# mLSTM output part on pairs of chunks, and the output projection in steps of 24 products

## The chip, the cores and the metric

The kernel runs on one core of one Trainium2 chip. The metric is device time in microseconds (us) of one execution, as the median of several runs. The five engines appear in the profile as PE (TensorE's matmuls) and PEld (its weight loads), DVE (VectorE), ACT (ScalarE), POOL (GpSimd) and SP (SyncE, which here only issues DMAs).

## What is computed

One encoder layer for two sequences, 2048 and 256 tokens, with model width 1024 and float32 data. An RMSNorm and one input projection feed two groups of heads: eight bidirectional mLSTM heads and eight attention heads (grouped, with two key heads). Their outputs stand side by side and pass through the output projection `w_out`, with a residual. Then follow a second norm, an up projection, a width-3 convolution, a gate and a down projection.

```python
x = x + jnp.concatenate([m_out, a_out], axis=-1) @ w_out
h = rmsnorm(x, norm2_w)
u = centred_dwconv(h @ w_up, conv_w, conv_b)
a, g = jnp.split(u, 2, axis=-1)
return x + (jax.nn.silu(g) * a) @ w_down
```

The change lies in the mLSTM heads. Per head and direction, with decay weights `Dw` inside a chunk and a carried state `C`, `n`:

```python
s = jnp.einsum('bhld,bhsd->bhls', qb, kb) * Dw
num = iw[..., None] * jnp.einsum('bhld,bhde->bhle', qb, C) + jnp.einsum('bhls,bhse->bhle', s, vb)
den = iw * jnp.einsum('bhld,bhd->bhl', qb, n) + jnp.sum(s, axis=-1)
h = num / jnp.maximum(jnp.abs(den), jnp.exp(-m_t))[..., None]
```

The two directions are added, each head is normalised by its root mean square, scaled, and multiplied by a sigmoid gate.

## The kernel before

Float32 products are made from two parts of each operand (a rounded high part and the rest), so one product of the text is three on TensorE. "Products" below are these single matmul instructions on 128 x 128 weights.

Tokens are cut into 18 chunks of 128 (`NT`) and 9 blocks of 256 (`NB`), so a block is a pair of chunks. `phase_a` (L139) norms the tokens and projects the attention heads, `gate_math` (L338) prepares the mLSTM gates. Then `run_both` (L1474) runs two Python generators against each other: `attention` (L430) and `mlstm` (L637). Each `yield` hands over a weight, and `run_both` takes the next step from the side that is behind by these weights. This gives the order in which instructions are emitted. The framework then orders them for each engine by priority (the place of emission, less the offset of a `high_priority` region) and by what is ready in its own timeline; on the chip every engine runs its instructions in that order.

`mlstm` goes over four pairs of heads, p = 0 to 3. For each, `proj_steps` (L846) makes keys, queries, values and gate of the nine blocks, two steps of 48 products each for a block, and writes the gate to `og_d`; `upd` (L751) makes the state increments, `recur` (L765) chains them over the chunks on VectorE, and `out_steps` (L862) makes the outputs. The output steps of pair p alternate with the projection steps of pair p + 1. For the last pair (p = `LASTP` = 3), the query and gate projection of a block, `proj_qo` (L725), is made inside `out_steps`, at every second chunk; its gate goes to one of three `ogT` tiles (`OTB`).

The output part of a chunk i has four pieces, all emitted at `high_priority` with an offset of 2000 (`MPRI`), but for the first:
- `out_a` (L774): GpSimd issues a DMA that broadcasts the chunk's row of `nm_d` into the tile `dm`, masks both directions with `affine_select` (L782), and ScalarE takes four exponentials of 128 x 128 (L785). For p < 3 it also loads the gate of a block (L790).
- `out_b` (L794): the score product `pS` (L799), two VectorE products with `dm` (L802), the state product `pI` (L805) and its scaling into `s1` (L808).
- `out_c` (L811): the value product `pN` (L817), added to `s1` (L818), three small denominator operations (L820 to L822), the normalisation (L823), the sum over directions into `hh` (L826), two squares on ScalarE that also overwrite part of `s1` (L829), the reciprocal root on GpSimd (L98, L99), the product with it (L831) and the gate (L833).
- `out_d` (L835): a transpose (L838), a scaled copy on ScalarE (L841; for p = 3 a product with the gate on VectorE, L843) and a DMA to `mix_d` (L844).

Step i of `out_steps` emits `out_d` of chunk i - 6, `out_c` of i - 2, `out_b` of i - 1 and `out_a` of i. There are three `dm` tiles (`DMB`), two `s1` tiles (`S1B`), six `hh` tiles (`DLAG`), and two PSUM banks (`MB`) for all small mLSTM products.

When `mlstm` has ended, its tiles are released and `phase_c` (L902), the output projection, is the second generator: four steps load and split `w_out`; then, for each block, four "z-steps" make 48 products each (`mm`, L935) and add the residual (`post`, L945). The norm of a block (`tail`, L953) is emitted at the first z-step of the next one. One step is taken at each attention step (`CSTEP`), and a block begins only when attention has finished its tokens (`g.mixed`). From then on attention is emitted at `high_priority` with an offset of 1000 (`APRI`). When attention has ended, the remaining steps of `phase_c` are run alone (L1455), and each of them releases one of seven preparations of the up projection: four sums of `n2` (`n2_sums`, L1023) and three operand loads (`n2_load`, L1001). The last block's norm is emitted after the first products of the up projection (L1466).

Of the kernel before, what the change touches and what calls it, by code (L numbers as in the profile page):

```python
# [9 lines left out]
F32 = mybir.dt.float32  # L10
F32R = mybir.dt.float32r
AF = mybir.ActivationFunctionType
ALU = mybir.AluOpType
# [4 lines left out]
P = 128  # L18
# [4 lines left out]
NT = T // P  # L23
# [5 lines left out]
NEG = -1e30  # L29
# [8 lines left out]
NB = T // BT  # L38
# [7 lines left out]
LASTP = 3  # L46
OW3 = 3
OTB = 3
# [8 lines left out]
RST = 512  # L57
QZB = 2
RWM = 4
S1B = 2  # L60
DMB = 3
KWB = 2
CSTEP = 1
TDVE = 6
# [15 lines left out]
P0 = ((V, V),) * 4  # L80
P1 = ((V, V),) * 7
LOP = ()
DLAG = 6
SEGS = ((0, NT1), (NT1, NT))


# [8 lines left out]
def rstd_of(g, pool, ms, n, name):  # L95
    nc = g.nc
    r = pool.tile([P, n], F32, tag="rstd", name=name)
    nc.gpsimd.tensor_scalar(r, ms, EPS, None, ALU.add)  # L98
    nc.gpsimd.tensor_tensor(r, r, g.mhalf[:, 0:n], ALU.pow)  # L99
    return r  # L100
# [536 lines left out]
def mlstm(g, tc, s1, sp, sw, sn, pj_, pm):  # L637


    nc = g.nc  # L640
# [3 lines left out]
    tm = g.tm  # L644
# [129 lines left out]
    def out_a(s, i):  # L774
        nm = f"{s.p}_{i}"
        o = Pair()
        o.dm = sp.tile([P, 2, 2, P], F32, tag="dm", name="dm" + nm, bufs=DMB)
        nc.gpsimd.dma_start(o.dm.rearrange("p d h l -> p (d h l)"),
                          g.nm_d[i, 4 * s.p:4 * s.p + 4].rearrange("r l -> (r l)").unsqueeze(0).to_broadcast([P, 4 * P]))
        for d in range(2):  # L780
            sgn = 1 - 2 * d
            nc.gpsimd.affine_select(out=o.dm[:, d], in_=o.dm[:, d], compare_op=ALU.is_ge, fill=NEG, base=0,  # L782
                                    pattern=[[0, 2], [sgn, P]], channel_multiplier=-sgn)
            for h in range(2):
                nc.scalar.activation(o.dm[:, d, h], o.dm[:, d, h], AF.Exp,  # L785
                                     bias=tm[:, i, 0, d, 2 * s.p + h:2 * s.p + h + 1])
        if s.p < LASTP:
            if i % 2 == 0:
                s.og = s1.tile([P, 2, P], F32, tag="ogT", name="ogr" + nm, bufs=OTB)
                nc.gpsimd.dma_start(s.og, g.og_d[s.p, i // 2])  # L790
            o.og = s.og[:, i % 2]
        return o

    def out_b(s, i, o):  # L794
        nm = f"{s.p}_{i}"
        pS = pm.tile([P, 2, P], F32, tag="m", name="mS" + nm)
        t = slice((i % 2) * P, (i % 2) * P + P)
        q = s.qb[i // 2][:, i % 2]
        nc.tensor.matmul(pS.rearrange("p h t -> p (h t)"), s.kT[i // 2][:, t], q.rearrange("p h t -> p (h t)"),  # L799
                         start=True, stop=True)  # L800
        for d in range(2):
            nc.vector.tensor_tensor(o.dm[:, d], o.dm[:, d], pS, ALU.mult)  # L802
        pI = pm.tile([P, 2, 2, 65], F32, tag="m", name="mI" + nm)
        for h in range(2):
            nc.tensor.matmul(pI[:, h].rearrange("p d e -> p (d e)"), q[:, h, :],  # L805
                             s.C[i].rearrange("p d e -> p (d e)"), start=True, stop=True)
        o.s1 = sp.tile([P, 2, 2, 65], F32, tag="s1", name="s1" + nm, bufs=S1B)
        nc.vector.tensor_tensor(o.s1, pI.rearrange("p h d e -> p d h e"),  # L808
                                tm[:, i, 2, :, s.hs].unsqueeze(3).to_broadcast([P, 2, 2, 65]), ALU.mult)

    def out_c(s, i, o):  # L811
        nm = f"{s.p}_{i}"
        s1 = o.s1
        pN = pm.tile([P, 2, 2, 65], F32, tag="m", name="mN" + nm)
        for d in range(2):
            for h in range(2):
                nc.tensor.matmul(pN[:, d, h, :], o.dm[:, d, h, :], s.va[i // 2][:, i % 2, h, :], start=True, stop=True)  # L817
        nc.vector.tensor_tensor(s1, pN, s1, ALU.add)  # L818
# [3 lines left out]
        nc.vector.reciprocal(dn, dn)  # L822
        nc.vector.tensor_tensor(s1[:, :, :, 0:64], s1[:, :, :, 0:64],  # L823
                                dn.unsqueeze(3).to_broadcast([P, 2, 2, 64]), ALU.mult)
        hh = o.hh = sp.tile([P, 2, 64], F32, tag="hh", name="hh" + nm, bufs=DLAG)
        nc.vector.tensor_tensor(hh, s1[:, 0, :, 0:64], s1[:, 1, :, 0:64], ALU.add)  # L826
        ms = sp.tile([P, 2], F32, tag="mms", name="mms" + nm, bufs=4)
        for h in range(2):
            nc.scalar.activation(s1[:, 0, h, 0:64], hh[:, h, :], AF.Square, scale=0.125, accum_out=ms[:, h:h + 1])  # L829
        r = rstd_of(g, sp, ms, 2, "mr" + nm)  # L830
        nc.vector.tensor_tensor(hh, hh, r.unsqueeze(2).to_broadcast([P, 2, 64]), ALU.mult)  # L831
        if s.p < LASTP:
            nc.vector.scalar_tensor_tensor(hh, o.og.rearrange("p (h d) -> p h d", h=2), 1.0, hh, ALU.add, ALU.mult)  # L833

    def out_d(s, i, o):  # L835
        nm = f"{s.p}_{i}"
        pT = pm.tile([P, P], F32, tag="m", name="mT" + nm)
        nc.tensor.transpose(pT, o.hh.rearrange("p h d -> p (h d)"), g.ident)  # L838
        mx = sp.tile([P, P], F32, tag="mmx", name="mmx" + nm, bufs=2)
        if s.p < LASTP:  # L840
            nc.scalar.activation(mx, pT, AF.Copy, scale=mhw[:, s.p:s.p + 1])  # L841
        else:
            nc.vector.tensor_tensor(mx, pT, s.og[i // 2][:, (i % 2) * P:(i % 2) * P + P], ALU.mult)  # L843
        (nc.scalar if s.p < LASTP else nc.sync).dma_start(g.mix_d[i // 2, :, s.p, (i % 2) * P:(i % 2) * P + P], mx)  # L844

    def proj_steps(s):  # L846
        for b in range(NB + 2):
# [14 lines left out]
    def out_steps(s):  # L862
        os_ = {}
        s.og = {}
        for i in range(NT + DLAG):
            if s.p == LASTP and i % 2 == 0 and i < NT:
                proj_qo(s, i // 2)
            if DLAG <= i:
                with tc.high_priority(offset=MPRI):
                    out_d(s, i - DLAG, os_.pop(i - DLAG))  # L870
            if 2 <= i < NT + 2:
                with tc.high_priority(offset=MPRI):
                    out_c(s, i - 2, os_[i - 2])
            if 1 <= i < NT + 1:
                with tc.high_priority(offset=MPRI):
                    out_b(s, i - 1, os_[i - 1])
            if i < NT:
                os_[i] = out_a(s, i)
            yield (2.7 if s.p < LASTP else OW3) if i < NT else 1

    s = weights(0)
    yield from proj_steps(s)
    for p in range(4):
# [3 lines left out]
        if p < 3:  # L887
# [4 lines left out]
            while True:  # L892
                a, b = next(outs, None), next(ps, None)
# [3 lines left out]
            s = s2  # L897
# [4 lines left out]
def phase_c(g, sn, sp, pp, wps):  # L902
# [3 lines left out]
    nc = g.nc  # L906
# [28 lines left out]
    def mm(b, z, mx):  # L935
        po = pp.tile([P, 2, BT], F32, tag="po", name=f"po{b}_{z}")
        for o in range(2):
            n = slice(((2 * z + o) % 4) * P, ((2 * z + o) % 4 + 1) * P)
            for c in range(NCC):
                for k, (a, h) in enumerate(((0, 0), (0, 1), (1, 0))):  # L940
                    nc.tensor.matmul(po[:, o], wo[c][z // 2][:, a, n], mx[c][:, h, :],  # L941
                                     start=(c == 0 and k == 0), stop=(c == NCC - 1 and k == 2))
        return po

    def post(b, z, x, po, acc):  # L945
# [22 lines left out]
    for b in range(NB):  # L968
        yield 2 * b
        x, mx = loads(b)  # L970
        for z in range(4):
            po = mm(b, z, mx)
            if z == 0:
                if prev is not None:
                    tail(*prev)
                acc = sp.tile([P, 2, BT], F32, tag="acc", name=f"cacc{b}", bufs=1)
            post(b, z, x, po, acc)
            if z < 3:
                yield None
        prev = (b, x, acc)  # L980
# [576 lines left out]
```

## Time and profile before

| what | value |
|---|---|
| median of 3 runs | 3376.03 us (3375.04 to 3377.26) |
| the profiled execution | 3379.7 us |
| its span, first to last instruction | 3378.0 us |
| mean granted TensorE clock | 0.988 |
| VectorE busy, whole span | 2453.2 us (73%) |
| mLSTM output part: first `pS` product, last store | 430.0 us, 1432.6 us |
| output projection: first and last product | 1437.9 us, 1870.6 us |

A row of a group names line, engine, operation, output and inputs, shape and count; after the first bar stand its busy us and the mean ns of one instruction, after the second the idle time of its engine just before it and what ended that. A row of waits names the waiting engine and line, then what released it: us in total, how often, the longest. In a timeline row stand the start, the duration, engine and line. Matmuls overlap on TensorE: one of 512 columns is shown as some 400 ns, though the next begins after 230 ns.

### The profile page before, as it was taken

To read this page: it belongs to the slowest core of one execution; us is meant where nothing else is said; L and a number is where in the kernel's file an instruction comes from. 1 tells how busy PE (TensorE), PEld (TensorE's weight loads), DVE (VectorE), ACT (ScalarE), POOL (GpSimd) and SP (SyncE) were. 2 spreads that over 40 slices of the span, in tenths; PEclk is the share of its full clock that TensorE was granted. 3 is DMA by queue.
4 is the path that set the end of the run, shared out by engine and by line. 5 is a ranking of instruction groups with operands and counts; after the bars stand their busy time and mean duration, and the time that the engine had idled before them with its cause. 6 is when DMAs were issued, how large, how long until landed. Compare 5 with 4: busy or idle time off the path is not lost.

```text
span 3378.0 us, 53454 instructions
## 1 busy us (share of the span) xinstructions
PE 3270.3 (97%) x19566; PEld 3035.8 (90%) x19566; DVE 2453.2 (73%) x3659; ACT 1989.0 (59%) x3706; POOL 692.6 (21%) x1072
## 2 busy tenths in 40 slices
PE   7989999999999999999999899999999999999998
PEld 6778888888888888788878899999999999999998
DVE  7874576666657668876665899998889888666664
ACT  4535666666566776655554555676667667554543
POOL 7774133322215323211112100000000000010201
PEclk9999999999999999999999999999999999999999
DMA  8766343343337343343225756677666657867663
GB/s 246 216 182 193 103 122 94 108 129 96 99 101 217 119 130 118 102 147 99 84 83 158 266 208 219 213 250 264 236 228 240 213 193 258 315 231 274 218 233 122
DMA packets 394551, 601.69 MB, mean 178 GB/s; under 512 B 31248, under 2 KB 255536, under 8 KB 394288
## 3 DMA queue, kind: packets, MB, share of 16 engines
q1 hardware_dynamic: 361232, 553.43, 49.0%
q0 software_dynamic: 11600, 33.04, 3.7%
q10 hardware_dynamic: 21456, 11.80, 1.2%
q8 instruction: 154, 2.52, 0.3%
q14 instruction: 109, 0.89, 0.1%
HBM read 434.23 MB, written 163.92 MB: 177 GB/s over the span
## 4 chain that ended last, share of the span: by engine, by line
PE 73%; issue 7%; ACT 5%; DVE 5%; POOL 5%; DMA 4%; SPq 0%; POOLq 0%; ACTq 0%; DVEq 0%
PE pa L1091 16%; PE pc L1091 8%; PE pf L1347 6%; PE po L941 5%; PE pb L1091 4%; PE mj L681 4%; PE ph L1347 3%; PE mv L691 3%; PE ps L553 3%; PE pv L570 3%; PE pv L572 3%; PE ps L554 2%; PE pv L571 2%; PE px L530 2%; PE pg L1347 2%
## 5 line engine op out<-in xcount | busy, mean ns | idle before, releaser
L559 DVE TENSOR_TENSOR xx<-pe,xx 128x1024 fp32r<-128x1024 f32 x260 | 322.9, 1242 | 193.6 <-ACT xx L558 191.9
L557 ACT ACTIVATE pe<-ps 128x1024 f32<-128x1024 f32 x260 | 266.1, 1023 | 225.2 <-PE ps L554 216.2
L532 DVE TENSOR_REDUCE mx<-px 128x1 f32<-128x1024 f32 x256 | 309.8, 1216 | 93.9 <-PE px L530 92.7
L1305 POOL TENSOR_TENSOR sq<-sq,sq 128x384 f32<-128x384 f32 x38 | 48.7, 1282 | 1397.6 <-ACT sq L1301 1315.8
L558 ACT ACTIVATE xx<-pe 128x1024 fp32r<-128x1024 f32 x260 | 274.9, 1058 | 6.3 <-PE pv L572 1.3
L941 PEld LDWEIGHTS po<-cmx,wo 128*128 128x128 f32 x1728 | 228.6, 191 | 18.2 <-ACT cmx L928 2.1
L941 PE MATMUL po<-cmx,wo 128*128 128x256 f32 x1728 | 235.8, 283 | 1.4 <-ACT cmx L928 1.1
L1095 ACT ACTIVATE u<-pa 128x386 f32<-128x386 f32 (+2 forms) x264 | 129.2, 489 | 177.7 <-PE pa L1091 176.4
L553 PE MATMUL ps<-qq,kk 128*128 128x512 f32 x520 | 214.4, 412 | 13.7 <-ACT pe L557 10.4
L570 PE MATMUL pv<-xx,vv 128*128 128x512 f32 x520 | 214.3, 412 | 13.7 <-ACT rs L580 7.8
L572 PE MATMUL pv<-xx,vv 128*128 128x512 f32 x520 | 212.6, 409 | 2.9 <-DVE xx L559 2.8
L571 PE MATMUL pv<-xx,vl 128*64 128x512 f32 x520 | 209.6, 403 | 0.0
L554 PE MATMUL ps<-qm,kl 65*128 65x512 f32 x520 | 208.5, 401 | 0.4 <-ACT qm L545 0.4
L681 PEld LDWEIGHTS mj<-mn,wm 128*128 128x128 f32 x1296 | 177.9, 193 | 16.8 <-ACT og L695 3.9
L691 PE MATMUL mv<-wm,mn 128*128 128x256 f32 x1296 | 192.2, 286 | 0.8 <-ACT qb L687 0.8
L681 PE MATMUL mj<-mn,wm 128*128 128x256 f32 x1296 | 190.2, 288 | 2.8 <-ACT og L695 2.4
L227 PE MATMUL pj<-w_a,n1T 128*128 128x512 f32 (+1 forms) x864 | 179.1, 362 | 10.7 <-DVE n1T L185 6.3
L691 PEld LDWEIGHTS mv<-wm,mn 128*128 128x128 f32 x1296 | 175.9, 190 | 14.1 <-ACT qb L687 1.4
L227 PEld LDWEIGHTS pj<-w_a,n1T 128*128 128x128 f32 x864 | 144.4, 196 | 31.0 <-DVE n1T L185 7.2
L530 PE MATMUL px<-kk,qq 128*128 128x512 f32 x512 | 165.9, 405 | 5.4 <-ACT pe L557 4.5
L785 ACT ACTIVATE dm<-dm,tm 128x128 f32<-128x128 f32 x288 | 95.0, 392 | 107.5 <-POOL dm L782 103.2
L1091 PE MATMUL pc<-nt,wb 128*128 128x386 f32 (+2 forms) x792 | 148.4, 341 | 4.8 <-ACT nt L1015 3.3
(325 smaller groups left out, 8314.5 us busy)
## 6 DMA issues: line engine op xcount, KB each, us to landing
mn<-n_d SPq DMA_DIRECT2D x216, 256.0 KB, 3.2
ru<-w_up SPq DMA_DIRECT2D x88, 512.0 KB, 5.1
rs<-wsu_d SPq DMA_DIRECT2D x88, 512.0 KB, 5.5
act_d<-ts SPq DMA_DIRECT2D x33, 768.0 KB, 5.8
nt<-act_d SPq DMA_DIRECT2D x60, 384.0 KB, 4.9
re_t<-wsd_d SPq DMA_DIRECT2D x45, 512.0 KB, 5.0
wsu_d<-tw SPq DMA_DIRECT2D x44, 512.0 KB, 3.9
act_d<-ya SPq DMA_DIRECT2D x99, 192.0 KB, 3.0
```

The lines of the kernel that those rows point to most:

```text
L227: nc.tensor.matmul(pjs[t][:, c0:c1], nTs[tiles[t]][:, c, a, :], ws[c][:, b, c0:c1], start=(c == 0 and k == 0), stop=(c == NCC - 1 and k == 2))
L532: nc.vector.tensor_reduce(s.mx[:, t0, z0:z0 + 1], ps, AX.X, ALU.max)
L553: nc.tensor.matmul(o, kk[:, kc:kc + P], s.qq, start=True, stop=False)
L559: nc.vector.tensor_tensor(x[:, 1], pe, f32(x[:, 0]), ALU.subtract)
L570: nc.tensor.matmul(s.pv, vv[:, kt % 4, :], x1, start=kt == 0, stop=False)
L571: nc.tensor.matmul(s.pv[0:HD], vl[:, kt % 4, :], x1, start=False, stop=False)
L572: nc.tensor.matmul(s.pv, vv[:, kt % 4, :], x2, start=False, stop=kt == s.nk - 1)
L681: nc.tensor.matmul(pj[:, o], s.w[c][:, a, o * P:(o + 1) * P], nT[c][:, h, :], start=(c + o + k == 0), stop=(c == NCC - 1 and k == 2 and o ...
L691: nc.tensor.matmul(pv[:, o], nT[c][:, a, o * P:(o + 1) * P], s.w[c][:, h, 256:512], start=(c + o + k == 0), stop=(c == NCC - 1 and k == 2 ...
L941: nc.tensor.matmul(po[:, o], wo[c][z // 2][:, a, n], mx[c][:, h, :], start=(c == 0 and k == 0), stop=(c == NCC - 1 and k == 2))
L1091: s.nc.tensor.matmul(p, w[:, aa, c, :], ops[k][:, c, bb, 0:s.n], start=c == 0 and i == 0 and not add, stop=c == NCC // 2 - 1 and i == 2, s ...
L1347: nc.tensor.matmul(ps[c], w[:, aa, c, :], t[:, gi - g0, bb, 0:H], start=gi == 0 and m == 0 and not more, stop=gi == NG - 1 and m == 2, ski ...
```

## The change

The four pieces of the output part take a block b (two chunks) where they took a chunk:
- `out_a`: `dm` holds two chunks; one DMA and one `affine_select` for each direction, over both chunks; eight exponentials as before; the gate load of the block.
- `out_b`: both chunks' `pS` products go to one bank, and one VectorE product of 1024 columns takes all of `dm`; `pI` and its scaling stay two.
- `out_c`: `pN` and its addition stay two; the denominator, normalisation, sum over directions, reciprocal root, product and gate are one operation each for the block; four squares as before.
- `out_d`: two transposes into one bank, one copy (or product) and one DMA of 256 columns.

Buffers: `s1` one of double size (was two), `dm` two of double size (were three), `hh` two of double size (were six), `mmx` one of double size (was two). `out_steps` emits `out_a` and, for p = 3, `proj_qo` of block 0 ahead of its loop; in a block's first half step `out_d` of j - 2, then `proj_qo` of j + 1, then `out_c` of j - 1; in its second half step `out_b` of j and `out_a` of j + 1. It yields twice per block with the weights as before (2.7, or 3 for the last pair), and with 1 in the two steps at the end.

In `phase_c`, `mm` yields after the first of its two groups of 24 products, so a block is handed out in eight steps.

```diff
-S1B = 2
-DMB = 3
+S1B = 1
+DMB = 2
-DLAG = 6
+DLAG = 2
...
-        for d in range(2):
-            nc.vector.tensor_tensor(o.dm[:, d], o.dm[:, d], pS, ALU.mult)
+        dm = o.dm.rearrange("p d i h l -> p d (i h l)")
+        nc.vector.tensor_tensor(dm, dm, pS.rearrange("p i t -> p (i t)").unsqueeze(1).to_broadcast([P, 2, 4 * P]),
+                                ALU.mult)
...
-        dn = sp.tile([P, 2, 2], F32, tag="dn", name="dn" + nm, bufs=4)
-        nc.vector.scalar_tensor_tensor(dn, s1[:, :, :, 64], -1.0, s1[:, :, :, 64], ALU.mult, ALU.max)
-        nc.vector.tensor_tensor(dn, dn, tm[:, i, 3, :, s.hs], ALU.max)
+        dn = sp.tile([P, 2, 2, 2], F32, tag="dn", name="dn" + nm, bufs=2)
+        nc.vector.scalar_tensor_tensor(dn, s1[:, :, :, :, 64], -1.0, s1[:, :, :, :, 64], ALU.mult, ALU.max)
+        nc.vector.tensor_tensor(dn, dn, tm[:, 2 * b:2 * b + 2, 3, :, s.hs], ALU.max)
         nc.vector.reciprocal(dn, dn)
...
-        for i in range(NT + DLAG):
-            if s.p == LASTP and i % 2 == 0 and i < NT:
-                proj_qo(s, i // 2)
+        last = s.p == LASTP
+        if last:
+            proj_qo(s, 0)
+        os_[0] = out_a(s, 0)
+        for j in range(NB + DLAG):
+            w = (OW3 if last else 2.7) if j < NB else 1
+            if DLAG <= j:
+                with tc.high_priority(offset=MPRI):
+                    out_d(s, j - DLAG, os_.pop(j - DLAG))
+            if last and j + 1 < NB:
+                proj_qo(s, j + 1)
+            if 1 <= j <= NB:
+                with tc.high_priority(offset=MPRI):
+                    out_c(s, j - 1, os_[j - 1])
+            yield w
+            if j < NB:
+                with tc.high_priority(offset=MPRI):
+                    out_b(s, j, os_[j])
+            if j + 1 < NB:
+                os_[j + 1] = out_a(s, j + 1)
+            yield w
...
                     nc.tensor.matmul(po[:, o], wo[c][z // 2][:, a, n], mx[c][:, h, :],
                                      start=(c == 0 and k == 0), stop=(c == NCC - 1 and k == 2))
+            if o == 0:
+                yield None
         return po
...
-            po = mm(b, z, mx)
+            po = yield from mm(b, z, mx)
```

More of the change, by code (lines that the diff above doesn't have):

```diff
@@ L792, in out_a @@
[L792 to L800, printed above, removed]
-        for d in range(2):
[L802 to L818, printed above, removed]
-        dn = sp.tile([P, 2, 2], F32, tag="dn", name="dn" + nm, bufs=4)
-        nc.vector.scalar_tensor_tensor(dn, s1[:, :, :, 64], -1.0, s1[:, :, :, 64], ALU.mult, ALU.max)
-        nc.vector.tensor_tensor(dn, dn, tm[:, i, 3, :, s.hs], ALU.max)
[L822 to L839, printed above, removed]
+            nc.gpsimd.affine_select(out=o.dm[:, d].rearrange("p i h l -> p (i h) l"),
+                                    in_=o.dm[:, d].rearrange("p i h l -> p (i h) l"), compare_op=ALU.is_ge, fill=NEG,
+                                    base=0, pattern=[[0, 4], [sgn, P]], channel_multiplier=-sgn)
@@ new lines, in out_a, with out_b @@
+            for i in range(2):
+                for h in range(2):
+                    k = 2 * s.p + h
+                    nc.scalar.activation(o.dm[:, d, i, h], o.dm[:, d, i, h], AF.Exp, bias=tm[:, i0 + i, 0, d, k:k + 1])
+        if s.p < LASTP:
+            o.og = s1.tile([P, 2, P], F32, tag="ogT", name="ogr" + nm, bufs=OTB)
+            nc.gpsimd.dma_start(o.og, g.og_d[s.p, b])
+        return o
+    def out_b(s, b, o):
+        nm = f"{s.p}_{b}"
+        pS = pm.tile([P, 2, 2 * P], F32, tag="m", name="mS" + nm)
+        for i in range(2):
+            nc.tensor.matmul(pS[:, i], s.kT[b][:, i * P:(i + 1) * P], s.qb[b][:, i].rearrange("p h t -> p (h t)"),
+                             start=True, stop=True)
+        dm = o.dm.rearrange("p d i h l -> p d (i h l)")
+        nc.vector.tensor_tensor(dm, dm, pS.rearrange("p i t -> p (i t)").unsqueeze(1).to_broadcast([P, 2, 4 * P]),
+                                ALU.mult)
+        o.s1 = sp.tile([P, 2, 2, 2, 65], F32, tag="s1", name="s1" + nm, bufs=S1B)
+        for i in range(2):
+            pI = pm.tile([P, 2, 2, 65], F32, tag="m", name=f"mI{nm}_{i}")
+            for h in range(2):
+                nc.tensor.matmul(pI[:, h].rearrange("p d e -> p (d e)"), s.qb[b][:, i, h, :],
+                                 s.C[2 * b + i].rearrange("p d e -> p (d e)"), start=True, stop=True)
+            nc.vector.tensor_tensor(o.s1[:, i], pI.rearrange("p h d e -> p d h e"),
+                                    tm[:, 2 * b + i, 2, :, s.hs].unsqueeze(3).to_broadcast([P, 2, 2, 65]), ALU.mult)
@@ L840, in out_d @@
+    def out_d(s, b, o):
+        nm = f"{s.p}_{b}"
+        pT = pm.tile([P, 2, P], F32, tag="m", name="mT" + nm)
+        for i in range(2):
+            nc.tensor.transpose(pT[:, i], o.hh[:, i].rearrange("p h d -> p (h d)"), g.ident)
+        mx = sp.tile([P, 2, P], F32, tag="mmx", name="mmx" + nm, bufs=1)
         if s.p < LASTP:
```

59 lines of the change are left out of this document (35 added, 24 removed).

## The prediction

> **What bounds the kernel now.** I read the page first (engine shares), then busy time by stretch (windows), the waits of TensorE, the groups by line, and last the timelines around the places where TensorE stands idle.
>
> ```profile
> span 3378.0 us, 53454 instructions
> PE 3270.3 (97%) x19566; PEld 3035.8 (90%) x19566; DVE 2453.2 (73%) x3659; ACT 1989.0 (59%) x3706; POOL 692.6 (21%) x1072
> ```
>
> TensorE is busy 97% of the span, so the whole kernel has 3378.0 - 3270.3 = 108 us in which it shows no work, and every term below is a share of that. The change touches the mLSTM stage (430 to 1437 us) and the output projection beside and behind attention (1437 to 1906 us). The columns of the next rows are the stretch, its length, then busy us of PE, PEld, DVE, ACT and POOL, the granted clock, and the share and GB/s of the DMA engines.
>
> ```profile
> 430.00:1220.00 790.00, 775.00 (x4882) 676.03 (x4881) 539.77 (x1020) 507.09 (x1187) 252.24 (x491) 0.99 0.38 117
> 1220.00:1437.00 217.00, 210.20 (x1263) 177.97 (x1262) 166.48 (x348) 145.48 (x329) 63.76 (x110) 0.99 0.40 121
> ...
> 1280.00:1330.00 50.00, 46.95 (x264) 38.92 (x262) 42.02 (x95) 33.01 (x78) 19.62 (x35) 0.97 0.32 92
> 1405.00:1455.00 50.00, 43.02 (x206) 30.86 (x204) 45.02 (x80) 39.06 (x73) 8.35 (x14) 1.00 0.41 131
> ...
> 1437.00:1630.00 193.00, 188.67 (x1228) 166.60 (x1227) 128.91 (x176) 105.87 (x161) 31.48 (x31) 1.00 0.36 119
> 1630.00:1656.00 26.00, 22.89 (x103) 17.21 (x102) 19.36 (x26) 13.18 (x17) 2.55 (x4) 0.87 0.30 97
> 1656.00:1736.00 80.00, 80.00 (x534) 71.76 (x533) 48.01 (x63) 42.01 (x60) 13.51 (x13) 1.00 0.25 81
> 1736.00:1806.00 70.00, 57.51 (x243) 41.45 (x242) 41.40 (x51) 43.82 (x59) 7.37 (x12) 0.91 0.16 46
> ...
> 1866.00:1906.00 40.00, 30.46 (x158) 29.08 (x157) 33.09 (x47) 18.71 (x25) 8.06 (x5) 0.83 0.93 327
> ```
>
> TensorE's idle time, length less busy: 15.0 + 6.8 = 21.8 us in the mLSTM stage; 4.3 + 3.1 + 0 + 12.5 = 19.9 us while attention runs beside the output projection; 9.5 us at the hand-over to the up projection. Where attention has products of another kind beside it (1656 to 1736) TensorE has no gap at all. Where it has none (1405 to 1455, 1736 to 1806) it loses 14% and 18%. So the ordinary products are filler, and the time is set by where filler is missing and by attention's own chain of waits there:
>
> ```profile
> PE ps L553 <- ACT pe L557: 5.1, 10, 1.6
> PE pv L570 <- ACT rs L580: 4.4, 5, 2.1
> PE px L530 <- ACT pe L557: 3.1, 3, 1.9
> PE pv L570 <- ACT xx L558: 2.5, 5, 0.7
> PE pv L572 <- DVE xx L559: 1.5, 4, 0.7
> ```
>
> These are TensorE's longest waits from 430 to 1437 us (total, times, longest). ScalarE ends most of them; VectorE directly ends 1.5 us. That already says that taking work off VectorE can't return its full amount.
>
> **VectorE, ScalarE and GpSimd work that is merged.** Rows of the operations concerned (busy us, mean ns of one after the bar):
>
> ```profile
> L559 DVE TENSOR_TENSOR xx<-pe,xx 128x1024 fp32r<-128x1024 f32 x260 | 322.9, 1242 | 193.6 <-ACT xx L558 191.9
> ...
> L802 DVE TENSOR_TENSOR dm<-dm,mS 128x256 f32<-128x256 f32 x144 | 53.6, 413 | 15.9 <-PE mS L799 15.0
> L823 DVE TENSOR_TENSOR s<-s,dn 128x256 f32<-128x256 f32 x72 | 31.0, 431 | 1.4
> L818 DVE TENSOR_TENSOR s<-mN,s 128x260 f32<-128x260 f32 x72 | 30.3, 420 | 12.3 <-PE mN L817 12.0
> L831 DVE TENSOR_TENSOR hh<-hh,mr 128x128 f32<-128x128 f32 x72 | 23.9, 331 | 47.3 <-POOL mr L99 45.7 <-ACT qb L687 1.0
> L826 DVE TENSOR_TENSOR hh<-s 128x128 f32<-128x128 f32 x72 | 22.9, 318 | 1.3
> L833 DVE SCALAR_TENSOR_TENSOR hh<-ogr,hh 128x128 f32<-128x128 f32 x54 | 16.1, 297 | 1.0
> L822 DVE RECIPROCAL dn<-dn 128x4 f32<-128x4 f32 x72 | 12.4, 172 | 1.3
> L946 DVE TENSOR_TENSOR cx<-po,cx 128x512 f32<-128x512 f32 x36 | 24.7, 686 | 31.0 <-PE po L941 30.9
> ...
> L829 ACT ACTIVATE s<-hh 128x64 f32<-128x64 f32 x144 | 35.2, 247 | 22.7 <-DVE hh L826 22.5
> L829 ACT ACTIVATION_READ_ACCUMULATOR s<-hh 128x1 f32 x144 | 27.3, 189 | 0.0
> ```
>
> For one pair of chunks of one head pair, of which there are 9 x 4 = 36: four dm products of 413 ns become one of 1024 columns, 1242 ns by the row of the same width, saving 410. The three small denominator operations stand twice each before; by the reciprocal's 172 ns they save 3 x 172 = 516. The normalisation (431 twice) becomes 512 columns, 686 ns: 176. The sum of directions (318 twice), the rstd product (331 twice) and the gate (297 twice; the last head pair has an output product there instead, taken alike) become 256 columns each, 425 ns as an estimate between the 413 and 431 of that width: 211, 237 and 169. The 420 ns operations on pI and pN stay two each. Sum 1.72 us, times 36 = 62 us of VectorE's 2453. [...]
>
> ScalarE keeps the eight exponentials per pair and the four squares; only out_d's copies merge, under 10 us in all. GpSimd's masks cover twice the columns in half the number, and two rstd operations per pair go; GpSimd is 21% busy and stays off the path. The dm loads stay two per pair with equal bytes, and the stores to mix_d halve in number. TensorE's products are the same, so it gains only idle time.
>
> What are 62 us of VectorE worth? At most TensorE's 21.8 us of idle, plus stalls too short to show beside pipelined products; at least nothing. The two stretches where VectorE is nearly full, 42.02 and 45.02 of 50 us, hold 3.0 + 7.0 = 10 us of that idle. I take half of it, 5 us, because attention's own operations fill the rest of VectorE there, and a quarter of the other 11.8, 3 us. **-8 us** (0 to -15).
>
> **The new order of the output part.** The last head pair's query and gate projection is handed out earlier: its ninth block now has 3 x 4 + 4 = 16 units of weight behind it (two steps of the block, two of the next, four of weight 1) where it had 2 x 3 + 6 = 12. A unit is 217 / 60 = 3.6 us, so the stretch without projection products before the output projection starts grows by some 14 us.
>
> ```profile
> L707 PE MATMUL mv<-mvn,wm x432: 274/283/472, 1219.7 to 1399.6; 128*128 128x256 f32 x144
> ...
> L941 PE MATMUL po<-cmx,wo x1728: 274/281/580, 1437.9 to 1870.6; 128*128 128x256 f32 x192
> ```
>
> Today that stretch lasts from 1400 to 1438 us, and it loses at the 14% worked out above: 14 us x 14% = **+2 us** (0 to +5).
>
> **The output projection in steps of 24.** Beside attention I take **0** (-12 to +4). The order on TensorE is not in blocks of 48 today:
>
> ```profile
> 1485.82 1.48 PE L941 MATMUL po<-cmx,wo 128*128 128x256 f32 x11
> 1487.14 0.62 PE L530 MATMUL px<-kk,qq 128*128 128x512 f32 x2
> 1487.60 1.47 PE L941 MATMUL po<-cmx,wo 128*128 128x256 f32 x11
> ```
>
> It is dealt out product by product into attention's gaps, because attention is emitted at a priority 1000 instructions ahead, and handing out smaller pieces changes nothing where it is filler already. The gates on finished attention tiles stay.
>
> Behind attention the hand-out does matter: the remaining steps each release one of seven preparations of the up projection (four n2 sums, three loads). Twice as many steps per block means these come at half the spacing, and begin some four z-steps earlier.
>
> ```profile
> 1812.70 0.93 SPq L1031 DMA_DIRECT2D rn<-n_d  x2
> ...
> 1852.39 1.31 SPq L1031 DMA_DIRECT2D rn<-n_d  x2
> ...
> 1870.60 0.37 SPq L1014 DMA_DIRECT2D nt<-n2t_d  x1
> ...
> PE rs_c L135 <- POOL rcol_c L133: 3.7, 1, 3.7
> PE pc L1091 <- ACT nt L1015: 3.3, 1, 3.3
> ```
>
> The sums now run from 1813 to 1852 us and the load behind them is issued at 1871, when the first up products already stand on TensorE. An earlier start would let those products fill the 3.7 us wait for the last norm. The 3.3 us wait is for a tile whose space is freed by that norm, and stays. **-3 us** (-7 to +2, since the sums then meet the loads of the last two blocks on SP's queue).
>
> **Sum.** -8 + 2 + 0 - 3 = -9 us. The profiled execution took 3379.7 us (1.7 outside the span), 3.7 above the median of the runs, 3376.03. 3379.7 - 9 = 3370.7 profiled, so **3367 us** as a median. 0.2%, 6.8 us, is about what a measurement of this kernel can tell from no change.
>
> **Rivals.** First: VectorE's relief is worth nothing, since ScalarE ends the waits, and the longer stretch takes back the little that the hand-over gives: 0 + 2 + 0 - 3 = -1, 3375 us. For it speaks the list of waits; against it, that VectorE is 84 to 90% busy just where TensorE idles.
>
> Second: the finer hand-out spreads the filler so that it lasts through 1630 to 1656 and 1736 to 1806, 3.1 + 12.5 us of idle. Four blocks take 16 attention steps before and 32 after, nearly the 36 steps of four head blocks. If 12 us of that come back: -9 - 12 = -21, 3355 us. The runs of eleven products speak against it.
>
> Third, slower: the single s1 buffer and the two pair-wide dm buffers make the output part one serial chain. The first write of s1 must wait for the four squares of the pair before, 4 x (247 + 189) = 1.74 us, and those for its whole VectorE chain: 1242 + 4 x 420 + 516 + 686 + 425 = 4.5 us, stretched by attention's operations in front of each. The last head pair's projection depends on this chain through the gate buffers. The pace there is 217 / 9 = 24 us for a pair, and the bare chain 6 us, so it decides only where queueing makes it three to four times as long. Then 100 us run as 1405 to 1455 does, at 14%: +14, with the tail's +2 and no gain elsewhere +16, 3392 us. A single wait is there today:
>
> ```profile
>   ACT s L829: 2.5, 2
> ```
>
> That is VectorE's idle time before s1's write, 2.5 us in two cases. [...]
>
> **Chances.** My forecast (3358 to 3369, faster) 0.39; the second rival 0.13, also faster: 0.52. The first, no change: 0.26. The third 0.22. The range leaves out the worst of the second and the upper part of the third: 3346 to 3390.
>
> **What would show it.** Right: the merged dm product near 1.24 us x36 and VectorE's busy time down by some 60 us; TensorE's products unchanged; its idle time from 430 to 1437 us falling from 21.8 to about 14, with the projection's last product some 10 us earlier relative to the first output product; the n2 sums done before 1840 and no 3.7 us wait at the hand-over. Wrong: runs of output products clearly shorter or longer than today and a filled stretch before attention's end (second rival); VectorE waiting on the squares dozens of times, or the output part's start-to-end growing (third); the same idle time with a lighter VectorE (first).

## The result, and the profile after

The changed kernel takes **3396.17 us** (median of 6 runs, 3391.09 to 3405.32). Beside it the kernel before took 3375.54 us (6 runs, 3374.30 to 3377.26). The ratio is 1.0063, with a 95% interval of 1.0049 to 1.0077: it is slower by some 20 us. I forecast 3367 us, faster, so the sign was wrong. The profiled execution took 3393.13 us, 13.4 more than the profiled one of before; the terms below are made against it.

The page after, its span and engines:

```profile
span 3391.4 us, 52630 instructions
PE 3275.4 (97%) x19566; PEld 3039.5 (90%) x19566; DVE 2415.5 (71%) x3299; ACT 1986.9 (59%) x3679; POOL 647.8 (19%) x928
```

VectorE has 37.7 us less to do and GpSimd 45, as the merge meant. Yet TensorE's idle time over the span, 3391.4 - 3275.4 = 116.0 us, is 8.3 more than before, and with the same 19566 products its busy time is 5.1 more. By stretch, with the columns of the prediction's rows:

```profile
430.00:1220.00 790.00, 765.86 (x4823) 670.08 (x4822) 502.76 (x746) 496.03 (x1147) 222.70 (x382) 0.98 0.41 117
1220.00:1437.00 217.00, 208.22 (x1254) 176.83 (x1253) 152.18 (x250) 140.63 (x328) 49.38 (x73) 0.98 0.42 119
```

In the mLSTM stage TensorE now idles 24.1 + 8.8 = **32.9 us** where it idled 21.8, and its granted clock is lower too. From 1437 to 1950 it idles 30.2 us after and 30.0 before, so the loss belongs to the stage before the output projection. TensorE's and VectorE's and ScalarE's waits in that stage (430 to 1437 us) show its kind. These are waits of the profile after:

```profile
PE pv L570 <- ACT rs L580: 6.3, 4, 2.4
...
PE mu L760 <- DVE s L812: 2.6, 1, 2.6
PE mT L849 <- DVE hh L840: 2.5, 3, 1.6
PE mT L849 <- DVE hh L843: 1.9, 1, 1.9
...
DVE s L823 <- PE mN L822: 40.4, 29, 5.6
DVE s L812 <- ACT s L836: 32.8, 12, 6.4
...
ACT dm L791 <- POOL dm L785: 90.5, 39, 7.0
```

The waits of TensorE that VectorE ends come to 12.7 us in the whole list after, and to 4.0 in the whole list of before (the five rows of the prediction show 1.5 of these). VectorE waits for the squares (L836) 32.8 us in 12 cases, where it was 2.5 in 2; this is what the third rival would look like. ScalarE waits for the masked `dm`, that is for a load. It did so before too, and for longer in all:

```profile
ACT dm L785 <- POOL dm L782: 103.2, 54, 7.1
```

So the sum of this wait does not tell what it costs; that depends on what stands behind it. One place shows how these hang together, in the timeline after:

```profile
1134.49 1.49 POOL L780 DMA_DIRECT2D dm<-nm_d  x2 [5.02 <-PE mt L741]
...
1139.98 0.64 POOL L785 TENSOR_SCALAR_AFFINE_SELECT dm<-dm 128x512 f32<-128x512 f32 x1 [3.89 <-DMA dm<-nm_d]
...
1140.65 1.28 ACT L791 ACTIVATE dm<-dm,tm 128x128 f32<-128x128 f32 x4 [5.66 <-POOL dm L785]
...
1142.36 1.28 ACT L791 ACTIVATE dm<-dm,tm 128x128 f32<-128x128 f32 x4 [0.43 <-POOL dm L785]
...
1143.55 0.24 ACT L836 ACTIVATE s<-hh 128x64 f32<-128x64 f32 x1
...
1144.63 0.77 DVE L812 TENSOR_TENSOR s<-mI,tm 128x260 f32<-128x260 f32 x2 [6.45 <-ACT s L836]
...
1145.20 0.46 PE L760 MATMUL mu<-va,kw 128*128 128x130 f32 x2 [2.64 <-DVE s L812]
...
1146.01 0.63 PE L553 MATMUL ps<-qq,kk 128*128 128x512 f32 x1
```

Read it from the end. TensorE stands 2.64 us for a PSUM bank, because VectorE has not yet read `mI` out of it. VectorE stands 6.45 us because the one `s1` tile is still written by the squares of the pair before. The squares stand on ScalarE behind eight exponentials, and the first of these waits 5.66 us for a `dm` mask. That mask waits for a load issued at 1134.5. So at this place a late load passes through four engines. The last row shows a second price: an attention product of 512 columns lasts 0.63 us where it lasts 0.40 otherwise. The clock has been halved behind the gap:

```profile
1135.00:1145.00 10.00, 7.56 (x54) 6.85 (x53) 3.44 (x10) 3.89 (x17) 2.60 (x7) 1.00 0.71 184
1145.00:1150.00 5.00, 4.80 (x22) 4.36 (x23) 2.96 (x7) 4.87 (x10) 2.25 (x4) 0.66 0.11 31
1150.00:1160.00 10.00, 10.00 (x61) 8.45 (x60) 6.71 (x7) 8.11 (x16) 2.15 (x4) 1.00 0.36 117
```

The trace's record of the granted clock has TensorE at half clock six times between 430 and 1437 us after, 30.7 us in all, and three times, 13.7 us, before. Behind the gap above, products of 512 columns begin 0.43 us apart (1146.01, 1146.44 and 1146.87 us), where they begin 0.23 to 0.24 us apart ahead of it. Half of the time at half clock, taken as lost, is an estimate from this: 15.4 us against 6.8.

Why are the loads late? Below are the rows of the DMA queue (packets, MB, the time that they took as a share of 16 engines) and of the `dm` loads (KB each, median us from issue to landing). Before:

```profile
q0 software_dynamic: 11600, 33.04, 3.7%
...
dm<-nm_d POOLq DMA_DIRECT2D x72, 256.0 KB, 3.8
```

After:

```profile
q0 software_dynamic: 11600, 33.04, 4.6%
...
dm<-nm_d POOLq DMA_DIRECT2D x72, 256.0 KB, 5.5
```

There are as many loads, packets and bytes, but a load lands 1.7 us later. The change's load takes one direction of two chunks: two pieces of 1 KB per partition that stand in `nm_d` at two places. The load before took 2 KB of one chunk in one piece. The prediction had written "two per pair with equal bytes" and looked no further.

A load can also be late because it is issued late. Before it may issue one, GpSimd stands 151.0 us in 26 cases for the products `pN` that free a `dm` tile (before: 182.0 us in 45). No run gives the pairs a third `dm` tile, so whether that would have hidden the later landing is open.

### The profile page after: what moved, and what is told of

The parts are those of the page before. It is cut to its first block, busy times and chain, and to the rows that moved or that the text cites. A ratio compares the mean times of both kernels' runs of the same rounds, so it can differ in the third digit from the quotient of the medians.

```text
span 3391.4 us, 52630 instructions
## 1 busy us (share of the span) xinstructions
PE 3275.4 (97%) x19566; PEld 3039.5 (90%) x19566; DVE 2415.5 (71%) x3299; ACT 1986.9 (59%) x3679; POOL 647.8 (19%) x928
## 4 chain that ended last, share of the span: by engine, by line
PE 80%; issue 4%; POOL 4%; DVE 4%; DMA 4%; ACT 3%; SPq 0%; POOLq 0%; ACTq 0%; DVEq 0%
PE pa L1110 16%; PE pc L1110 8%; PE pf L1366 7%; PE po L958 6%; PE ph L1366 4%; PE mv L691 4%; PE pb L1110 4%; PE ps L553 3%; PE ps L554 3%; PE pv L570 3%; PE pv L572 3%; PE mj L681 3%; PE pv L571 3%; PE px L530 3%; PE pg L1366 2%
## 5 line engine op out<-in xcount | busy, mean ns | idle before, releaser
L570 PE MATMUL pv<-xx,vv 128*128 128x512 f32 x520 | 213.8, 411 | 15.2 <-ACT rs L580 8.2
L1110 PEld LDWEIGHTS pc<-nt,wb 128*128 128x128 f32 x792 | 141.7, 191 | 10.0 <-ACT nt L1034 9.5
```

What stands on the lines that cost most here:

```text
L570: nc.tensor.matmul(s.pv, vv[:, kt % 4, :], x1, start=kt == 0, stop=False)
L1110: s.nc.tensor.matmul(p, w[:, aa, c, :], ops[k][:, c, bb, 0:s.n], start=c == 0 and i == 0 and not add, stop=c == NCC // 2 - 1 and i == 2, s ...
```

## The experiments

All ratios are to the kernel before, run beside it on the same chip, with 95% intervals. "Idle" is TensorE's idle time from 430 to 1437 us in the profiled execution. This window is fixed, while the first output product starts between 1400.5 us (e13) and 1468.0 us (e3), so it compares the stage only roughly.

| run | median us | ratio | idle |
|---|---|---|---|
| before | 3375.54 | | 21.8 |
| the change | 3396.17 | 1.0063 (1.0049 to 1.0077) | 32.9 |
| e1_pairs48 | 3395.70 | 1.0063 (1.0039 to 1.0087) | 32.7 |
| e2_half | 3372.72 | 0.9995 (0.9984 to 1.0005) | 21.8 |
| e3_junk | 3399.99 | 1.0071 (1.0050 to 1.0093) | 35.0 |
| e4_dma2k | 3355.73 | 0.9942 (0.9923 to 0.9962) | 17.8 |
| e5_dma1k | 3378.12 | 1.0007 (0.9997 to 1.0017) | 26.6 |
| e6_b1k | 3360.05 | 0.9959 (0.9945 to 0.9973) | 17.7 |
| e7_dma48 | 3357.44 | 0.9951 (0.9935 to 0.9968) | 18.1 |
| e8_junk_dma | 3351.80 | 0.9938 (0.9920 to 0.9956) | 20.6 |
| e9_before_l129 | 3373.64 | 0.9998 (0.9986 to 1.0009) | 21.4 |
| e10_before_l131 | 3377.07 | 0.9998 (0.9986 to 1.0010) | 20.0 |
| e11_after_l129 | 3397.44 | 1.0058 (1.0040 to 1.0076) | 32.0 |
| e12_after_l131 | 3389.47 | 1.0034 (1.0020 to 1.0048) | 33.7 |
| e13_dir2k | 3348.74 | 0.9910 (0.9893 to 0.9926) | 12.5 |
| e14_laydir | 3394.39 | 1.0053 (1.0032 to 1.0074) | 32.7 |
| e15_b1k_l129 | 3352.84 | 0.9925 (0.9910 to 0.9940) | 16.0 |
| e16_dma1k_l129 | 3377.26 | 0.9998 (0.9989 to 1.0007) | 25.5 |
| e17_dirsrc | 3366.92 | 0.9973 (0.9964 to 0.9982) | 16.5 |

### Which part of the change: e1_pairs48 and e2_half

Three theories stood at first. A: the single `s1` buffer ties VectorE to squares that queue behind exponentials. B: the new order of emission. C: the finer hand-out hurts at the hand-over. e1 is the change without its last part, e2 is the kernel before with that part alone:

```diff
-            if o == 0:
-                yield None
...
-            po = yield from mm(b, z, mx)
+            po = mm(b, z, mx)
```

> The pairs of chunks alone; the output projection is handed out in steps of 48 as before. Theory A (the slowdown comes from the mLSTM output part: the single s1 buffer ties VectorE to ScalarE's squares, which queue behind exponentials that wait for the dm loads): as slow as the change, 3388 to 3402 us. Theory C (the slowdown comes from the finer hand-out and what it does at the hand-over to the up projection): back to 3370 to 3382 us. Theory B (the order of emission of the output part as such, no single wait): as A here.

> The hand-out in steps of 24 products alone, the mLSTM output part as before. Theories A and B: within 7 us of before, 3369 to 3383 us, and the output products beside attention stand in the same runs as before. Theory C: 3388 us or more.

e1 is as slow as the whole change, and e2 is no different from before. So the 20 us are the pairs, and C falls.

### Is it the s1 buffer: e3_junk

```diff
-                nc.scalar.activation(s1[:, i, 0, h, 0:64], hh[:, i, h, :], AF.Square, scale=0.125,
+                nc.scalar.activation(junk, hh[:, i, h, :], AF.Square, scale=0.125,
```

> The change, but the squares of out_c write into a tile of their own, so that s1 is free when VectorE has summed the directions, and not when ScalarE has squared. Theory A: VectorE's wait for the squares ahead of s1's scaling (32.8 us in the change) is gone and 8 to 20 us come back, 3376 to 3388 us. Theories B and C: within 6 us of the change, 3390 to 3402 us.

The wait for the squares is gone from VectorE's list, and the time is no better. Another wait has grown in its place (it was 40.4 us); e3's waits of VectorE, 430 to 1437 us:

```profile
DVE s L823 <- PE mN L822: 50.8, 35, 5.5
DVE hh L841 <- POOL mr L99: 31.8, 17, 7.5
DVE C L771 <- ACT C L763: 23.6, 11, 4.2
DVE s L812 <- PE mI L810: 21.8, 14, 3.0
```

The squares were a place where lateness showed, not its source. Theory A falls as far as the buffer goes.

### Is it the loads: e4_dma2k, e7_dma48 and e8_junk_dma

e4 orders the `dm` tile chunk, direction, head, and loads a chunk's 2 KB at once, as before. The merged operations stay.

```diff
-        for d in range(2):
-            nc.gpsimd.dma_start(o.dm[:, d].rearrange("p i h l -> p i (h l)"),
-                                g.nm_d[i0:i0 + 2, 4 * s.p + 2 * d:4 * s.p + 2 * d + 2].rearrange("i r l -> i (r l)")
-                                .unsqueeze(0).to_broadcast([P, 2, 2 * P]))
+        for i in range(2):
+            nc.gpsimd.dma_start(o.dm[:, i].rearrange("p d h l -> p (d h l)"),
+                                g.nm_d[i0 + i, 4 * s.p:4 * s.p + 4].rearrange("r l -> (r l)").unsqueeze(0).to_broadcast([P, 4 * P]))
...
```

> The change, but with the two chunks as the outer index of dm, so that each dm load brings one chunk in runs of 2 KB, as before the change, instead of one direction of two chunks in runs of 1 KB. The merged operations stay merged. Theory A: loads land after 3.8 us again instead of 5.5, the squares and the s1 write move ahead, 4 to 12 us come back, 3384 to 3392 us. Theories B and C: landing shorter, time within 6 us of the change, 3390 to 3402 us.

> e4_dma2k with the output projection handed out in steps of 48 products as before: in the mLSTM stage its instructions stand in the same order as e4's, and only the projection behind it differs. Theory D (and A): 3352-3360 us, as e4, since the 24 steps alone gave nothing in e2_half (0.9995); e4's gain shows in the mLSTM stage again. If e4's time was luck of one placement: anything from 3360 up. Theory C (the finer steps cost at the hand-over): under 3350 us.

> e4_dma2k with the squares of the normalisation written into a tile of their own, so that s1 comes free without ScalarE (as e3_junk did to the change). Theory D: VectorE's wait at s on the squares (27.8 us in e4) goes, but it was cover, not cause, once the loads land early: 3350-3360 us. Theory A (the single s1 buffer costs TensorE time of its own): 3335-3350 us.

e4 turns the change from 20 us slower into 20 us faster than before. No expectation had this: theory A, the one that went by the landing, had said 4 to 12 us, and 40 came. e7 agrees with it at 48 products per step, so the gain lies in the mLSTM stage and the steps of 24 matter as little there. e8, with the squares' own tile as well, gives 3351.80 us, with an interval that overlaps e4's: once the loads come early, the buffer costs little or nothing.

### How short are the runs: e5_dma1k, e6_b1k, e15_b1k_l129, e16_dma1k_l129

Two unused columns in the tile (e4's in e5, the old kernel's in e6) cut the same loads into runs of 1 KB. e15 is e6, and e16 is e5, with LEAD at 1.29 (below). The edit of e6 against the kernel before:

```diff
-        o.dm = sp.tile([P, 2, 2, P], F32, tag="dm", name="dm" + nm, bufs=DMB)
+        o.dm = sp.tile([P, 2, 2 * P + 2], F32, tag="dm", name="dm" + nm, bufs=DMB)[:, :, 0:2 * P].rearrange("p d (h l) -> p d h l", h=2)
...
```

> The kernel e4_dma2k (merged operations, one dm load per chunk) with two unused columns behind each direction's 256 in the dm tile, so that the same loads of 256 KB leave in runs of 1 KB, not 2 KB; nothing else in the code differs, and the computation is whole. Theory D (the 1 KB runs of the change's loads make the dm tiles land late, the exponentials wait for them on ScalarE, and what queues behind them holds TensorE): the landing goes from e4's median 3.8-4.4 us back to 5-5.5 us, the issue on GpSimd from 546 to about 700 ns, and the time from 3355.7 to 3380-3400 us. Rival E (what e4 gained is the layout of the tile by chunk, one load per chunk with both directions in it, or the order that came with it, and not the runs): 3350-3365 us although the landing is late again.

> The kernel before, chunk by chunk, with its dm tile padded in the same way, so that its loads leave in runs of 1 KB; nothing else in the code differs, and the computation is whole. Theory D: the landing goes from 3.8 to 5-5.5 us and the time up by 5-20 us, to 3380-3395 us (three dm tiles of one chunk give the loads more lead than the change's two of a pair, so less than the change lost against e4). Rival E: 3372-3380 us, no different from before.

> e6_b1k (the kernel before with runs of 1 KB) with LEAD at 1.29. Were the 15 us that e6 gained on before an order that it happened to get, this goes back towards 3370-3380 us; if the padded tile or its loads do it whatever the order, 3355-3364 us.

> e5_dma1k (e4 with runs of 1 KB) with LEAD at 1.29. Theory R: 3370-3385 us again, 15-25 us above e4. If e5's loss of 22 us was an order that it happened to get: under 3368 us.

These were a bad test of theory D. The columns split the loads in SBUF alone; in DRAM the piece stays whole, and the landing hardly moves. e5, then e6:

```profile
dm<-nm_d POOLq DMA_DIRECT2D x72, 256.0 KB, 4.4
```

```profile
dm<-nm_d POOLq DMA_DIRECT2D x72, 256.0 KB, 4.0
```

e4 has 4.4 as well. What the columns do move is GpSimd's time to issue a load (e4 546 ns, e5 733, as in the change 737), and the order of the instructions, presumably because the framework orders them by its own estimate of a load. The two kernels went opposite ways, e5 22 us up from e4 and e6 15 us down from before, which neither expectation of e6 had, and both stay there or go further in e16 and e15. So D as I had put it, by the length of the runs alone, falls. Whether issue or order makes e5's 22 us and e6's 15 us is left open.

### Is it an order by chance: e9 to e12

```diff
-LEAD = 1.3
+LEAD = 1.29
```

> The kernel before with the planner's constant LEAD at 1.29 in place of 1.30: no instruction is other in kind, but from the mLSTM projection on thousands of them stand at other places in the engines' orders. It says how much of a difference of some 20 us the order alone can make. e6_b1k (runs of 1 KB, and 15 us faster than before) took theory D in its plain form away. Theory L (every edit reshuffles the order that the framework writes, and the shuffle is worth up to some 20 us either way): 3355-3395 us, and over 8 us from before. Theory M (the order moves little, and the differences between the kernels are those of their operations): 3370-3381 us.

> As e9_before_l129, with LEAD at 1.31. Theory L: 3355-3395 us, over 8 us from before or from e9_before_l129; theory M: 3370-3381 us.

> The change with LEAD at 1.29 in place of 1.30, again a reshuffle alone. Theory M (the change's own operations cost the 20 us, wherever they stand): 3388-3405 us, and 15-25 us above e9_before_l129. Theory L (the 20 us are the order that it happened to get): 3355-3390 us, and the difference to e9_before_l129 is another one, of either sign.

> The change with LEAD at 1.31. Theory M: 3388-3405 us, 15-25 us above e10_before_l131. Theory L: 3355-3390 us, and another difference to e10_before_l131.

The kernel before stays within 3 us, the change within 7, and the change is slower by 12 to 24 us in each pairing. Theory M is nearer. This shuffle is mild, though: by the traces 1 to 3% of TensorE's products stand in another sequence, while the columns moved some 11% in e5 and 12% in e6 (the fewest products to move from one sequence to the other, by the names of their tiles). It does not exclude that the order which the framework writes for a split load is what costs.

### Layout, landing or order: e13_dir2k, e14_laydir, e17_dirsrc

e14 has e4's tile with the change's loads by direction. e13 has the change's loads and masks, but `nm_d` is stored by pairs and the tile ordered to match, so that a load is one piece of 2 KB on both sides (the store of `nm_d` and the product's other factor follow that order):

```diff
-        dram("nm_d", [NT, 16, P])
+        dram("nm_d", [NB, 16, 2, P])
...
-            nc.gpsimd.dma_start(o.dm[:, d].rearrange("p i h l -> p i (h l)"),
...
+            nc.gpsimd.dma_start(o.dm[:, d].rearrange("p h i l -> p (h i l)"),
+                                g.nm_d[b, 4 * s.p + 2 * d:4 * s.p + 2 * d + 2].rearrange("r i l -> (r i l)")
+                                .unsqueeze(0).to_broadcast([P, 4 * P]))
...
```

> The change with its loads by direction kept, but nm_d stored by pairs in DRAM (both chunks of a row beside each other) and the dm tile ordered direction, head, chunk to match, so that each load of a direction is one run of 2 KB; the product's other factor is written in that order too. The computation is whole. Theory R (the short runs of the change's loads cost its 20 us): the landing falls from 5.5 to under 4.5 us, and the time to 3350-3365 us, as e4_dma2k. Theory Y (what e4 gained is the tile and load by chunk: both directions' masks wait for both loads, so that the eight exponentials come in one piece): 3385-3400 us, as the change, though the landing is short. In between, both.

> e4_dma2k with its tile by chunk kept and the loads by direction, as in the change (two runs of 1 KB each, from two chunks' places). Theory R: the landing goes to 5-5.5 us, and the time to 3380-3400 us. Theory Y, as far as it is the tile's order in SBUF: 3350-3365 us; as far as it is which load feeds which mask: 3385-3400 us, with R.

e14 is as slow as the change, though its tile is e4's: the layout by chunk is not the reason. e13 has the lowest median of the study, though it keeps loads and masks by direction; its load lands in 3.7 us. Theory Y falls, and R agrees. The loads of e14, with two pieces in DRAM, then of e13, with one:

```profile
dm<-nm_d POOLq DMA_DIRECT2D x72, 256.0 KB, 5.4
```

```profile
dm<-nm_d POOLq DMA_DIRECT2D x72, 256.0 KB, 3.7
```

The order was still another in e13. e17 settles that. Its source pieces stand side by side in DRAM, but go to two places of 1 KB in SBUF as in e14, and this leaves e14's order (which is the change's) in place on TensorE, VectorE and ScalarE but for the preparation of `nm_d`: by the traces 3 of TensorE's 19566 products stand elsewhere, and no instruction of VectorE or ScalarE. GpSimd still takes 737 ns to issue a load. The edit against e14:

```diff
-                                g.nm_d[i0:i0 + 2, 4 * s.p + 2 * d:4 * s.p + 2 * d + 2].rearrange("i r l -> i (r l)")
+                                g.nm_d[b, 2 * s.p + d].rearrange("i h l -> i (h l)")
...
```

> e14_laydir with nm_d stored in DRAM so that a load's two pieces stand beside each other there; in SBUF they still go to two places of 1 KB. The computation is whole. On VectorE, ScalarE and TensorE the instructions stand in the change's own order (e14's order is the change's on every engine, instruction for instruction; here the transposes that make nm_d, 13 more small writes of it on SP and one step's place on GpSimd differ), so this changes what the loads take on the chip and not the order around them. Theory R (late landing on the chip costs the time): the landing falls from 5.4 to about 4.4 us, GpSimd's issue stays at 735 ns, and the time falls by 15 us or more, to 3355-3378 us. Theory O (the landing matters little; the framework takes the split load to be longer, and the order that it writes for such a load costs the time, in e5_dma1k too): 3388-3402 us at the short landing.

The same order with earlier loads takes 3366.92 us, 27 us less than e14 and 29 less than the change. Theory O falls for the greater part. e17's page and loads, its stretches, and the waits of VectorE and ScalarE:

```profile
span 3363.3 us, 52650 instructions
PE 3262.5 (97%) x19566; PEld 3032.3 (90%) x19566; DVE 2421.1 (72%) x3299; ACT 1985.9 (59%) x3679; POOL 657.2 (20%) x928
...
q0 software_dynamic: 11600, 33.04, 3.5%
...
dm<-nm_d POOLq DMA_DIRECT2D x72, 256.0 KB, 4.0
```

```profile
430.00:1220.00 790.00, 780.97 (x4993) 686.34 (x4992) 521.74 (x772) 516.05 (x1200) 235.82 (x393) 1.00 0.41 123
1220.00:1437.00 217.00, 209.50 (x1246) 176.07 (x1246) 170.38 (x270) 148.30 (x321) 46.97 (x65) 0.99 0.44 137
```

```profile
DVE s L812 <- ACT s L836: 18.9, 9, 4.1
...
ACT dm L792 <- POOL dm L787: 56.6, 31, 6.5
```

The same two waits in e14:

```profile
ACT dm L790 <- POOL dm L785: 98.6, 39, 7.4
...
DVE s L810 <- ACT s L834: 31.8, 11, 6.4
```

1.4 us less per load than e14 takes ScalarE's wait for the masks from 98.6 us (90.5 in the change) to 56.6, and VectorE's for the squares from 31.8 (32.8 in the change) to 18.9. Against the change the span is 28.1 us shorter: 15.2 less idle time (116.0 to 100.8) and 12.9 less busy time with the same products. The second term is for the most part the clock: TensorE is at half clock for 64.9 us where it was 88.7 (some 10 us at the very end of the span left out in both), and half of the 23.8 us, by the estimate above, is 11.9.

e13 is another 18 us faster than e17. Its issue is shorter (552 ns), its landing 0.3 us shorter and its order another (some 8% of TensorE's products); these three were not told apart.

## Why the prediction was wrong, point by point

- **VectorE's relief.** Two of the merged rows of the profile after:

```profile
L804 DVE TENSOR_TENSOR dm<-dm,mS 128x1024 f32<-128x1024 f32 x36 | 43.7, 1215 | 14.1 <-PE mS L801 13.8
L829 DVE TENSOR_TENSOR s<-s,dn 128x512 f32<-128x512 f32 x36 | 25.9, 720 | 1.0
```

  The forecast was 1242 and 686 ns. By the nine rows that were merged VectorE is relieved of 52 us (188.9 to 136.8), by its busy time of 37.7; I had said 62. The gain of 8 us at TensorE was not there in the change. Where the loads come early TensorE does idle less, 16.5, 17.8 and 12.5 us in e17, e4 and e13, against 21.8 before and "about 14" in the forecast. But that VectorE's relief does this is not shown: e6 and e15, the kernel before with two unused columns and nothing merged, idle 17.7 and 16.0 us and take 3360.05 and 3352.84 us, with VectorE as busy as before. That e17's 3366.92 us meets my 3367 is luck. e6, 430 to 1437 us, and ScalarE's wait for the masks in it:

```profile
430.00:1437.00 1007.00, 989.27 (x6193) 859.45 (x6192) 717.52 (x1378) 659.29 (x1525) 319.46 (x602) 1.00 0.40 118
...
ACT dm L785 <- POOL dm L782: 125.9, 61, 7.2
```

- **The step that failed** stands in the part on ScalarE and GpSimd: "The dm loads stay two per pair with equal bytes", at no cost. A load took 5.5 us in place of 3.8, and that cost 29 us (the change against e17), more than the whole forecast gain. I had not quoted the loads' row at all, and I had put the later landing at nothing without a reason. Why the pairs pass a late mask on to TensorE is open beyond the place at 1145 us: e6 lets ScalarE stand even longer for its masks, 125.9 us, and is faster than before.
- **The third rival** (0.22) had the sign and, at 3392 us, nearly the time. Its mechanism, the single `s1` buffer and the queueing before the squares, was seen as described (12 waits, 32.8 us), but e3 and e8 show that the buffer was where the lateness passed, not where it began. The rival's other half, the two pair-wide `dm` tiles, was not tested.
- **The longer stretch without projection products** came as said. The last projection product starts at 1390.9 and the first output product at 1448.1; these 57.2 us lose 5.4, where 38.3 us lost 3.1: +2.3 us against a forecast of 2. The closeness is partly luck: the stretch grew by 19 us and not by 14, and it loses 8 to 9%, not the 14% that I had taken from 1405 to 1455 us, a window that reaches 17 us into the output projection.
- **The steps of 24 beside attention**: 0 was right (e2, 0.9995). From 1437 to 1950 us nothing was won, so the second rival was wrong.
- **The hand-over**, -3 us, did not come. In e2 the sums come earlier (the last load for one is issued at 1822.9 us, not 1852.4), and the wait of 3.7 us for the norm is down to 0.6, as forecast, but the wait behind it grew from 3.3 to 7.2 us (in the change to 9.2). e2's waits of TensorE:

```profile
PE pc L1093 <- ACT nt L1017: 7.2, 1, 7.2
PE pa L1093 <- ACT wb L1065: 2.8, 1, 2.8
PE rs_c L135 <- POOL rcol_c L133: 0.6, 1, 0.6
```

  One wait had taken the place of the other, because the last norm's way through memory ends the stretch either way: in e2 its store is issued from 1873.7 us, the load of `nt` from 1882.8, and TensorE goes on at 1889.0.

## What to carry to other kernels

When an edit regroups a load, count its pieces on the DRAM side, not its bytes, and look at who stands behind it in order: here 1.7 us per load passed from ScalarE's queue to TensorE. Store an intermediate in the order in which it will be read; that made the same merge 9 us faster than before (e17, in the change's own order), where the load in two pieces made it 20 us slower. Test a merge against the unmerged kernel under more than one order of instructions: e6 gained 15 us with no merge at all. A waiting engine that holds another up may itself be waiting: taking away the nearest wait (e3) moved it and changed nothing.

## What the runs showed of the hardware

- **Pieces in DRAM.** At 256 KB and the same number of packets, the loads' landing was 5.4 to 5.5 us with two separate source pieces of 1 KB per row of the load (the change 5.5, e14 5.4), and 3.7 to 4.5 with one piece of 2 KB, whether it went to one place in SBUF (before 3.8, e4 4.4, e8 4.5, e13 3.7) or two (e5 4.4, e6 and e17 4.0).
- **GpSimd's issue** follows pieces on either side: 546 to 600 ns for one piece on both (before 600, e4 546, e13 552), 733 to 776 with two on one side or both (the change 737, e5 733, e6 776, e14 and e17 737).
- **The clock behind a stall.** Gaps of 2.64 and 2.26 us on TensorE in the change were each followed by 3.4 us at half clock, while one of 2.38 us (at 1401 us) was not, so the length of the gap alone does not decide. Over the span from the change to e17 the clock gave back almost as much as the idle time (11.9 us by the estimate above, and 15.2 us).
